# Loading q of the attention in one array over all partitions, q and k by token halves, and sharing the k split between engines

## The chip, the core and the metric

The kernel runs on one core of one Trainium2 chip. The metric is the device time of one execution in microseconds (us), lower is better; runs of a changed kernel are taken beside runs of the kernel before on the same chip, and a ratio below 1 means faster. The engines are TensorE (PE in the profile, PEld for its weight loads), VectorE (DVE), ScalarE (ACT), GpSimd (POOL) and SyncE (SP), which here only issues DMAs.

## The reference

One decoder block over 2048 tokens and 1024 channels, in float32. What matters here:

```python
proj = x @ w_in + b_in          # q, k, v for 3 head groups of 8 heads of 64; gates; LRU input; merge gates
q, k = rope(q), rope(k)
for g, (window, dilation) in enumerate(((128, 1), (512, 4), (2048, 16))):
    o_g, lse_g = dilated_band_attention(q[:, :, g], k[:, :, g], v[:, :, g], window, dilation)
attn = sum over g of softmax(lse)_g * o_g;   y_a = (attn * silu(g_attn)) @ w_attn_proj
y_b  = (rg_lru(causal_conv(u)) * silu(g_lru)) @ w_lru_proj
out  = (sigmoid(gA) * y_a + sigmoid(gB) * y_b) @ w_out + b_out
x    = layer_norm(alpha * x + out)
```

In `dilated_band_attention` the tokens are regrouped by their residue modulo the dilation, and each block of 128 queries meets the keys of its own block and of the block before it, under a band mask.

## The kernel before, in words

There are three stages, and all of them share the DMA queue that SP feeds.

**Stage A, the projection** (to 1473 us in the profile). The plan has 72 entries, two token halves times 36 pairs of 128 output features. All but the first entry of each half are computed by seven block products (`product`, line 595), one for each tick; a tick is 12 matmuls of 512 columns and 2.7 us of PE. Every fp32 operand is split in a rounded part (ACT) and a remainder (DVE or POOL), so a product needs three matmuls for each block. Raw weights are loaded by SP (lines 218 and 298 and others), the remainders of the weights are stored in the first half (`wl_scr`) and loaded again in the second (line 278). Finished tiles go through generators, "chains", which are resumed tick by tick while a budget for each engine lasts. `qk_chain` applies the rotary embedding and writes k to `k_scr` (line 315) and q, scaled and split, to `qh_scr` and `ql_scr` (line 326 for group 2, whose tokens are regrouped by 16, line 329 for the others). `v_chain` transposes v and writes it to `v_scr` (line 358 and those around it). For each of 12 units (a group `g` and a head pair `hp`) the arrays `qh`, `ql` and `k` are [128, 2048], the first head in rows 0 to 63, the second in rows 64 to 127.

**Stage B, the attention** (1473 to about 1804 us). `unit(u)` takes the groups in the order 0, 2, 1 for each head pair. Each of 12 units has 16 steps, 192 in all. In loop step `m` the kernel issues `step_s(m)` (scores `s`, line 966, then the masked row minimum on DVE, line 970, and exp on ACT, line 972), `step_t(m-3)` (transposes, line 981, copied out by ACT or DVE, lines 986 and 988) and `step_v(m-4)` (times V, line 1005). The result goes to `o_scr` from ACT's DMA queue every four steps. Scores have three PSUM buffers, so `step_s(3)` waits for the exp input of step 0 to have been read.

The operands of a unit are prepared by `unit_parts(u)`:

- `A` is q: for head `h` one half of the partitions holds the rounded part and the other the remainder. It takes four loads (`q_part`, line 798) of 64 partitions with 8 KB each.
- `C` (named `b2` in the code) receives k, one load of 64 partitions for each head (`k_part`, line 777); its other partitions stay zero (memsets on POOL, lines 773 and 774, in units 0 and 1).
- `B` (`B1`) gets the rounded k in both halves of the partitions, two copies, and `C` keeps the remainder, one subtraction. This "split" is done for each head and each half of the tokens, [64, 1024] each. Only for head 0 of unit 0 do ACT (lines 781 and 782) and DVE (line 788) do it; everything else is done by POOL (lines 785, 786, 788).

A function `later(n, fn)` puts work off by n ticks or steps; the splits come 3 and 4 after the load. `first` is `unit_parts(0)`, `second` is `unit_parts(1)`, `firstv` is `v_parts(0, 0)`, the V of group 0 for the first two head pairs. In the last entry of stage A, whose seven ticks are j = 0 to 6, these loads are issued as the buffers of stage A come free: k of unit 0 at j = 2, q at j = 3, V at j = 4, k of unit 1 at j = 5 and 6. After stage A come the rest of `second` and the V of group 2; from then on one load is issued for each step, those of unit u+1 from the first step of unit u on (`loads`).

The order on each engine is the order in which the program issues. The layer below gives the DMAs of SP and ACT in turn one of eight counters, and a DMA waits until the one before it on its counter has landed. So SP, which works in order, can be held by a DMA that was issued eight places earlier, and that may be one of ACT's.

**Stage C, the combination and the output projections**, follows and is not touched.

Of the kernel before, what the change touches and what calls it, by code (L numbers as in the profile page):

```python
# [8 lines left out]
F32 = mybir.dt.float32  # L9
# [6 lines left out]
P = 128  # L16
S = 2048
# [3 lines left out]
CH = 512  # L21
# [10 lines left out]
def hybrid_block_kernel(ctx: ExitStack, tc: tile.TileContext, a: dict, out: bass.AP):  # L32
    nc = tc.nc
    sp, act, dve, pool, pe = nc.sync, nc.scalar, nc.vector, nc.gpsimd, nc.tensor

    def flat(t):
        return t.bitcast(F32)


    dram = ctx.enter_context(tc.tile_pool(name="dram", bufs=1, space=DRAM))  # L40
# [5 lines left out]
    mg_scr = dram.tile([2 * D, S], F32, name="mg_scr")  # L46
    yb_scr = dram.tile([D, S], F32, name="yb_scr")

    v_scr = [[dram.tile([S, 260], F32, name=f"v_scr{g}{j}") for j in range(2)] for g in range(3)]

    qk_scr = {(n, u): dram.tile([P, S], F32, name=f"{n}_scr{u}") for u in range(12) for n in ("qh", "ql", "k")}


    wl_scr = [dram.tile([P, 7, CH], F32, name=f"wl_scr{p}") for p in range(36)]
# [32 lines left out]
    def later(lag, fn):  # L87
        late.append((now["n"] + lag, fn))
# [201 lines left out]
    def qk_chain(rw, f, c):  # L290
        isq = f < FT_K
        u = f % 12
        g = u // 4
        nm = f"{f}_{c}"
        yield Ask(need=1)
        sw = take("sw" + nm)
        for b in range(4):
            sp.dma_start(flat(sw)[32 * b:32 * b + 32], flat(rw)[32 * (b ^ 1):32 * (b ^ 1) + 32])
        yield Ask(lag=2, DVE=1.2 if c < 2 else 1.0, POOL=1.7)
        cos, sin = CS[c % 2]  # L300
        tt(dve, flat(rw), flat(rw), cos, ALU.mult)
        tt(pool, flat(sw), flat(sw), sin, ALU.mult)
        yield Ask(lag=1, need=1 if g else 0, DVE=1.2 if g else 1.0)
        if g == 0:
            rp = rw
            tt(dve, flat(rp), flat(rw), flat(sw), ALU.add)
            give(sw)
        else:
            rp = take("rp" + nm)
            v, r = "p (j r) -> p j r", 4 if g == 1 else 16  # L310
            tt(dve, blocks(flat(rp), g), flat(rw).rearrange(v, r=r), flat(sw).rearrange(v, r=r), ALU.add)
            give(rw, sw)
        if not isq:
            yield Ask()
            sp.dma_start(qk_scr["k", u][:, c * CH:(c + 1) * CH], flat(rp))
            give_sent(rp)
            return
        yield Ask(need=1, ACT=.66, DVE=.9)
        hi = take("hi" + nm)
        act.activation(hi, flat(rp), AF.Copy, scale=0.125)  # L320
        dve.scalar_tensor_tensor(out=rp, in0=flat(rp), scalar=0.125, in1=flat(hi), op0=ALU.mult, op1=ALU.subtract)
        yield Ask()
        for t, part in ((hi, "qh"), (rp, "ql")):
            dst = qk_scr[part, u]
            if g == 2:
                sp.dma_start(dst.rearrange("p (r i) -> p r i", r=16)[:, :, 32 * c:32 * c + 32],
                             flat(t).rearrange("p (r i) -> p r i", r=16))
            else:
                sp.dma_start(dst[:, c * CH:(c + 1) * CH], flat(t))
        give_sent(hi, rp)  # L330


# [6 lines left out]
    def v_chain(vt, sgn, f, c):  # L339
        g, hp = divmod(f - FT_V, 4)  # L340
        st = {}

        def turn():
            tp = st["tp"] = ps.tile([P, 4, P], F32, tag="t", name=f"vtp{f}_{c}", bufs=2)
            for b in range(4):
                pe.transpose(tp[:, b, :], flat(vt)[:, b * P:(b + 1) * P], ident)  # L346
            give(vt)

        yield Ask(cond=lambda: tog["n"] < 2)
        tog["n"] += 1  # L350
        pe_later(2, turn)
        yield Ask(lag=3, cond=lambda: len(vs_free) > 0, ACT=.66)
        vs = vs_free.pop(0)
        act.activation(vs[:, :, 1:129], st["tp"], AF.Copy, scale=sgn)
        tog["n"] -= 1
        yield Ask()
        dst = v_scr[g][hp // 2][c * CH:(c + 1) * CH, (hp % 2) * 130:(hp % 2) * 130 + 130]
        sp.dma_start(dst.rearrange("(b p) f -> p b f", p=P), vs)
        vs_free.append(vs)


# [315 lines left out]
    for s, pl in enumerate(plan):  # L677
        if pl[0] and pl[4] == "ug":
            i = pl[1][1][0] - FT_U
# [69 lines left out]
    lo_, up_ = slice(0, 64), slice(64, P)  # L749
# [5 lines left out]
    units = {}  # L755
# [5 lines left out]
    def unit_parts(u):  # L761

        sl = USLOT[u % 2]
        g, hp = unit(u)
        q = {n: qk_scr[n, 4 * g + hp] for n in ("qh", "ql", "k")}

        def k_part(h, hs, os):
            def fn():
                if h == 0:
                    units[u] = [None, big(sl[1], [P, 2, S], F32R, f"B{u}")]  # L770
                    if u < 2:
                        B2[u] = big(sl[2], [P, 2, S], F32R, f"C{u}")
                        pool.memset(flat(B2[u][up_, 0]), 0.0)
                        pool.memset(flat(B2[u][lo_, 1]), 0.0)
                    units[u].append(B2[u % 2])
                _, B1, b2 = units[u]
                sp.dma_start(flat(b2[hs, h]), q["k"][hs])

                def split(t):
                    if (u, h) == (0, 0):  # L780
                        act.activation(B1[hs, h, t], flat(b2[hs, h, t]), AF.Copy)
                        act.activation(B1[os, h, t], flat(B1[hs, h, t]), AF.Copy)
                        eng = dve
                    else:
                        pool.tensor_copy(B1[hs, h, t], flat(b2[hs, h, t]))
                        pool.tensor_copy(B1[os, h, t], flat(B1[hs, h, t]))
                        eng = pool
                    eng.tensor_tensor(out=b2[hs, h, t], in0=flat(b2[hs, h, t]), in1=flat(B1[hs, h, t]), op=ALU.subtract)

                later(3, lambda: split(slice(0, S // 2)))  # L790
                later(4, lambda: split(slice(S // 2, S)))
            return fn

        def q_part(hs, h, n, qs):
            def fn():
                if (hs, h) == (lo_, 0):
                    units[u][0] = big(sl[0], [P, 2, S], F32R, f"A{u}")
                sp.dma_start(flat(units[u][0][hs, h]), q[n][qs])
            return fn

        return [k_part(0, lo_, up_), k_part(1, up_, lo_), q_part(lo_, 0, "qh", lo_), q_part(up_, 0, "ql", lo_),
                q_part(lo_, 1, "ql", up_), q_part(up_, 1, "qh", up_)]

    VT = {}

    def v_parts(g, j):
        src = v_scr[g][j]

        def part(i):
            def fn():  # L810
                if i == 0:
                    VT[g, j] = big(VSLOT[g, j], [P, 16, 260], F32, f"V{g}{j}")
                V = VT[g, j]
                if g == 0:
                    sp.dma_start(V[:, 4 * i:4 * i + 4], src[i * CH:(i + 1) * CH].rearrange("(n p) f -> p n f", p=P))
                elif g == 1:
                    sp.dma_start(V[:, 4 * i:4 * i + 4], src[i * CH:(i + 1) * CH].rearrange("(j r) f -> j r f", r=4))
                else:
                    sp.dma_start(V[:, 4 * i:4 * i + 4], src.rearrange("(i r) f -> i r f", r=16)[:, 4 * i:4 * i + 4])
            return fn  # L820

        return [part(i) for i in range(4)]
# [72 lines left out]
    first, second, firstv = unit_parts(0), unit_parts(1), v_parts(0, 0)  # L895
    low = NS
    where = [(s, j) for s in range(NQ) for j in range(ticks[s])]
    for T, (s, j) in enumerate(where):
        now["n"] = T
        for k in ("PE", "ACT", "DVE", "POOL"):  # L900
            left[k] = min(left[k], 0.0) + LEN
        if plan[s][2]:
            spend(**COST[plan[s][2][j]])
        product(s, j)
        for fn in events.pop(T, []):
            fn()
        run(late)
        run_chains()
        if s == NQ - 1:
            for fn in ((), (), first[:2], first[2:], firstv, second[:1], second[1:2])[j]:  # L910
                fn()
        evacuate(s, j)
        low = min(low, len(vacant))
        if TRACE:
            print(T, s, j, plan[s][4], len(vacant), len(lo_vacant), len(chains), {k: round(v, 1) for k, v in left.items()})
    n = len(where)
# [111 lines left out]
    def split(h, l, r, scale=None, eng=dve):  # L1028
        if scale is None:
            act.activation(h, r, AF.Copy)  # L1030
            eng.tensor_tensor(out=l, in0=r, in1=flat(h), op=ALU.subtract)
        else:
            act.activation(h, r, AF.Copy, scale=scale)
            dve.scalar_tensor_tensor(out=l, in0=r, scalar=scale, in1=flat(h), op0=ALU.mult, op1=ALU.subtract)
# [18 lines left out]
        later(1 if c else 2, lambda: split(t[:, 0], t[:, 1], r, eng=eng))  # L1053

    NB = 12 * 16
    for fn in second[2:] + v_parts(2, 0):
        fn()
    VORD = {0: (1, 0), 4: (0, 1), 5: (2, 1), 6: (1, 1)}
    loads = []
    for m in range(NB + 4):  # L1060
        u, n = divmod(m, 16)
# [142 lines left out]
    for n in range(32):  # L1204
        c, f = divmod(n, 8)
# [201 lines left out]
```

## Time and profile before

| | |
|---|---|
| runs | 2287.06 us median of 3 (2281.97 to 2290.84) |
| profiled execution | 2284.91 us |
| its span, first to last instruction | 2282.8 us |
| mean granted TensorE clock | 0.988 |
| PE, PEld busy | 2219.8 us (97%), 1870.6 us (82%) |
| DVE, ACT, POOL busy | 1743.3 us (76%), 1094.8 us (48%), 872.3 us (38%) |
| moved by DMA | 515.53 MB, mean 226 GB/s |

The busy share is an average over three stages. PE is the engine with the least idle time in stages A and B, so what matters is where PE is idle or slowed there, and what ended each of those waits. "Granted clock" is the share of full speed at which PE was allowed to run in a stretch.

### The profile page before, as it was taken

To read this page: it belongs to the slowest core of one execution; us is meant where nothing else is said; L and a number is where in the kernel's file an instruction comes from. 1 tells how busy PE (TensorE), PEld (TensorE's weight loads), DVE (VectorE), ACT (ScalarE), POOL (GpSimd) and SP (SyncE) were. 2 spreads that over 40 slices of the span, in tenths; PEclk is the share of its full clock that TensorE was granted. 3 is DMA by queue.
4 is the path that set the end of the run, shared out by engine and by line. 5 is a ranking of instruction groups with operands and counts; after the bars stand their busy time and mean duration, and the time that the engine had idled before them with its cause. 6 is when DMAs were issued, how large, how long until landed. Compare 5 with 4: busy or idle time off the path is not lost.

```text
span 2282.8 us, 34216 instructions
## 1 busy us (share of the span) xinstructions
PE 2219.8 (97%) x11008; PEld 1870.6 (82%) x11008; DVE 1743.3 (76%) x3228; ACT 1094.8 (48%) x1979; POOL 872.3 (38%) x640
## 2 busy tenths in 40 slices
PE   7999999999999999999999999989999999989998
PEld 6888878888888788888888888889999877768886
DVE  8787988999898777777878878656666578747677
ACT  5344545555455555565576565556666511121100
POOL 1544554556553012212312312465766256512220
PEclk9999999999999999999999999999999999999999
DMA  7998988988988777777777876995976589864431
GB/s 229 264 265 249 246 258 243 284 256 265 276 253 287 240 209 223 208 221 228 223 212 225 246 218 221 259 242 140 259 206 159 167 267 297 272 213 162 157 120 65
DMA packets 327443, 515.53 MB, mean 226 GB/s; under 512 B 96864, under 2 KB 137824, under 8 KB 322656
## 3 DMA queue, kind: packets, MB, share of 16 engines
q1 hardware_dynamic: 296352, 468.30, 66.5%
q0 software_dynamic: 10080, 18.35, 5.0%
q10 hardware_dynamic: 20832, 26.68, 3.6%
q8 instruction: 88, 1.44, 0.3%
q14 instruction: 91, 0.75, 0.1%
HBM read 307.89 MB, written 180.16 MB: 214 GB/s over the span
## 4 chain that ended last, share of the span: by engine, by line
PE 75%; DMA 7%; DVE 7%; issue 6%; ACT 2%; POOL 2%; SPq 1%; ACTq 0%; DVEq 0%; POOLq 0%
PE q L595 55%; PE o L1005 4%; PE s L966 3%; PE pt L981 2%; DMA A<-qh_scr 2%; PE z L1287 1%; PE z L1286 1%; PE z L1285 1%; PE yb L1194 1%; PE yb L1195 1%; PE yb L1193 1%; POOL me L1259 1%; PE vtp L346 1%; ACT p L972 1%; PE g L467 1%
## 5 line engine op out<-in xcount | busy, mean ns | idle before, releaser
L595 PE MATMUL q<-xT,hS 128*128 128x512 f32 x1680 | 521.1, 392 | 6.0 <-ACT e L618 6.0
L595 PE MATMUL q<-xT,l 128*128 128x512 f32 x1120 | 437.2, 390 | 0.0
L595 PE MATMUL q<-xB,hA 128*128 128x512 f32 x1248 | 389.5, 394 | 9.9 <-ACT xB L199 5.8
L595 PEld LDWEIGHTS q<-xT,hS 128*128 128x128 f32 x1680 | 315.1, 188 | 71.5 <-ACT e L618 6.4
L595 PE MATMUL q<-xB,l 128*128 128x512 f32 x904 | 354.0, 392 | 0.0
L595 PEld LDWEIGHTS q<-xB,hA 128*128 128x128 f32 x1248 | 235.2, 189 | 60.3 <-ACT xB L199 5.8
L595 PEld LDWEIGHTS q<-xT,l 128*128 128x128 f32 x1120 | 210.8, 188 | 44.4
L972 ACT ACTIVATE p<-p,osb 128x256 f32<-128x256 f32 (+1 forms) x384 | 156.6, 455 | 117.5 <-DVE osb L970 116.6
L211 POOL TENSOR_TENSOR S<-S,wA 128x512 f32<-128x512 f32 x35 | 45.7, 1305 | 424.4 <-DVE S L211 300.9
L970 DVE CUSTOM_DVE_ANT_0 p<-s,mask 128x256 f32<-128x256 f32 (+1 forms) x384 | 125.5, 364 | 101.8 <-PE s L966 65.5
L595 PEld LDWEIGHTS q<-xB,l 128*128 128x128 f32 x904 | 170.7, 189 | 36.2 <-DVE l L211 0.3
L211 POOL TENSOR_TENSOR sw<-sw,sin 128x512 f32<-128x512 f32 x96 | 160.2, 1675 | 65.4 <-DMA sw<-y 64.6
L595 PE MATMUL q<-xB,hS 128*128 128x512 f32 x560 | 173.9, 392 | 3.0 <-DVE v L211 3.0
L595 PE MATMUL q<-xT,hA 128*128 128x512 f32 x560 | 173.0, 390 | 1.5 <-ACT hi L320 1.3
L1005 PE MATMUL o<-V,ptb 128*128 128x65 f32 x1200 | 166.8, 278 | 7.4 <-ACT ptb L986 4.1
L1005 PEld LDWEIGHTS o<-V,ptb 128*128 128x128 f32 x1200 | 154.0, 197 | 18.5 <-ACT ptb L986 14.9
L256 ACT ACTIVATE hA<-wA 128x512 fp32r<-128x512 f32 x218 | 135.6, 624 | 68.1 <-DMA wA<-in_w_in_dram 21.3
L256 ACT ACTIVATE hS<-S 128x512 fp32r<-128x512 f32 x175 | 109.2, 624 | 102.3 <-DVE S L211 56.6
L211 POOL TENSOR_TENSOR l<-wA,hA 128x512 fp32r<-128x512 f32 x68 | 106.3, 1563 | 81.6 <-ACT hA L256 64.9
L966 PE MATMUL s<-B,A 128*128 128x256 f32 (+1 forms) x384 | 118.6, 330 | 8.3 <-DMA A<-qh_scr 5.7
L595 PEld LDWEIGHTS q<-xT,hA 128*128 128x128 f32 x560 | 104.8, 188 | 24.4 <-ACT hi L320 1.7
L595 PEld LDWEIGHTS q<-xB,hS 128*128 128x128 f32 x560 | 104.1, 188 | 24.7 <-issue 3.8
(196 smaller groups left out, 4843.7 us busy)
## 6 DMA issues: line engine op xcount, KB each, us to landing
wA<-in_w_in_dram SPq DMA_DIRECT2D x253, 256.0 KB, 4.9
wl_scr<-l SPq DMA_DIRECT2D x105, 512.0 KB, 5.2
l<-wl_scr SPq DMA_DIRECT2D x105, 512.0 KB, 4.5
sw<-y SPq DMA_DIRECT2D x384, 64.0 KB, 3.1
wS<-in_w_in_dram SPq DMA_DIRECT2D x70, 256.0 KB, 4.6
wS<-in_w_in_dram POOLq DMA_DIRECT2D x70, 256.0 KB, 6.6
o_scr<-osb ACTq DMA_DIRECT2D x48, 264.0 KB, 5.5
oc<-o_scr SPq DMA_DIRECT2D x48, 264.0 KB, 5.3
```

Source lines behind the costliest of these rows:

```text
L211: eng.tensor_tensor(out=out, in0=in0, in1=in1, op=op)
L256: act.activation(h, r, AF.Copy)
L346: pe.transpose(tp[:, b, :], flat(vt)[:, b * P:(b + 1) * P], ident)
L467: pe.matmul(g, gw[:, 1, j], vh, start=False, stop=True)
L595: pe.matmul(bank, w[:, ks], x[:, kk, xx], start=(first and i == 0), stop=(last and i == 11))
L966: pe.matmul(s[:, h, (0 if g == 2 and n else lo):256], q, k, start=(i == 0), stop=(i == 1))
L970: dve.tensor_tensor_reduce(out=p[:, h, lo:256], in0=s[:, h, lo:256], in1=mask[:, lo:256], scale=1.0, scalar=3e38, op0=ALU.add, op1=ALU.min ...
L972: act.activation(p[:, h, lo:256], p[:, h, lo:256], AF.Exp, scale=-1.0, bias=mm)
L981: pe.transpose(pt[:, 2 * h + x, :], p[:, h, x * P:(x + 1) * P], ident)
L1005: pe.matmul(o[:, n % 2, h * 65:h * 65 + 65], ptb[:, 2 * h + x, :], V[:, kb, vo + h * 65:vo + h * 65 + 65], start=(x == lo // P), stop=(x = ...
L1193: pe.matmul(yb, WL[f][:, 0, k], xx[:, 0], start=(k == 0), stop=False)
L1194: pe.matmul(yb, WL[f][:, 0, k], xx[:, 1], start=False, stop=False)
```

## The change

Three arrays and their loads are laid out anew, and the loads before stage B are issued in another order.

- q of a unit is one array `q_scr[u]` of [2, 128, 2048]: for each head the 128 rows as `A` wants them. `qk_chain` writes each tile into two row groups of 64. The rounded part goes to groups 0 and 3, the remainder to groups 1 and 2. For group 2 that takes two DMAs for each tile, one for each head, where it was one.
- `q_part(h, t)` loads all 128 partitions of one head and one half of the tokens (4 KB in each partition), four loads for each unit as before. `k_part(h, t)` loads one head and one half of the tokens, so k takes four loads where it took two. All of the first half of the tokens of k come first, then the second half, then q in the same order.
- The split of a half follows its own load by 3, and for both of the first two units ACT and DVE do head 0, both halves.
- V of group 0 is kept as [128, 16, 260], by key within the block and block, so that a load of four blocks is 4160 contiguous bytes in each partition, where it was four pieces of 1040.
- In the last entry of stage A the first loads start at j = 1, and k of unit 1 is issued between the V loads of unit 0.

```diff
-    v_scr = [[dram.tile([S, 260], F32, name=f"v_scr{g}{j}") for j in range(2)] for g in range(3)]
+    v_scr = [[dram.tile([S, 260] if g else [P, 16, 260], F32, name=f"v_scr{g}{j}") for j in range(2)] for g in range(3)]
-    qk_scr = {(n, u): dram.tile([P, S], F32, name=f"{n}_scr{u}") for u in range(12) for n in ("qh", "ql", "k")}
+    k_scr = [dram.tile([P, S], F32, name=f"k_scr{u}") for u in range(12)]
+    q_scr = [dram.tile([2, P, S], F32, name=f"q_scr{u}") for u in range(12)]
...
         for t, part in ((hi, "qh"), (rp, "ql")):
-            dst = qk_scr[part, u]
+            dst = q_scr[u].rearrange("h (x d) s -> (h x) d s", x=2)
+            dst = dst[0:4:3] if part == "qh" else dst[1:3]
             if g == 2:
-                sp.dma_start(dst.rearrange("p (r i) -> p r i", r=16)[:, :, 32 * c:32 * c + 32],
-                             flat(t).rearrange("p (r i) -> p r i", r=16))
+                src = flat(t).rearrange("p (r i) -> p r i", r=16)
+                for h in range(2):
+                    sp.dma_start(dst[h].rearrange("d (r i) -> d r i", r=16)[:, :, 32 * c:32 * c + 32],
+                                 src[64 * h:64 * h + 64])
             else:
-                sp.dma_start(dst[:, c * CH:(c + 1) * CH], flat(t))
+                sp.dma_start(dst[:, :, c * CH:(c + 1) * CH], flat(t))
...
-        def k_part(h, hs, os):
+        def k_part(h, t):
+            hs, os = ((lo_, up_), (up_, lo_))[h]
...
-                sp.dma_start(flat(b2[hs, h]), q["k"][hs])
-
-                def split(t):
-                    if (u, h) == (0, 0):
+                sp.dma_start(flat(b2[hs, h, t]), k[hs, t])
+
+                def split():
+                    if u < 2 and h == 0:
                         act.activation(B1[hs, h, t], flat(b2[hs, h, t]), AF.Copy)
                         act.activation(B1[os, h, t], flat(B1[hs, h, t]), AF.Copy)
                         eng = dve
...
-                later(3, lambda: split(slice(0, S // 2)))
-                later(4, lambda: split(slice(S // 2, S)))
+                later(3, split)
...
-        def q_part(hs, h, n, qs):
+        def q_part(h, t):
...
-                sp.dma_start(flat(units[u][0][hs, h]), q[n][qs])
+                sp.dma_start(flat(units[u][0][:, h, t]), q[h][:, t])
...
-        return [k_part(0, lo_, up_), k_part(1, up_, lo_), q_part(lo_, 0, "qh", lo_), q_part(up_, 0, "ql", lo_),
-                q_part(lo_, 1, "ql", up_), q_part(up_, 1, "qh", up_)]
+        T2 = (slice(0, S // 2), slice(S // 2, S))
+        return [k_part(h, t) for t in T2 for h in range(2)] + [q_part(h, t) for t in T2 for h in range(2)]
...
-                    sp.dma_start(V[:, 4 * i:4 * i + 4], src[i * CH:(i + 1) * CH].rearrange("(n p) f -> p n f", p=P))
+                    sp.dma_start(V[:, 4 * i:4 * i + 4], src[:, 4 * i:4 * i + 4])
...
-            for fn in ((), (), first[:2], first[2:], firstv, second[:1], second[1:2])[j]:
+            for fn in ((), first[:2], first[2:6], first[6:] + firstv[:1], firstv[1:2] + second[:2], firstv[2:3] + second[2:4], firstv[3:])[j]:
...
-    for fn in second[2:] + v_parts(2, 0):
+    for fn in second[4:] + v_parts(2, 0):
```

More of the change, by code (lines that the diff above doesn't have):

```diff
@@ L314, in qk_chain @@
             yield Ask()
-            sp.dma_start(qk_scr["k", u][:, c * CH:(c + 1) * CH], flat(rp))
+            sp.dma_start(k_scr[u][:, c * CH:(c + 1) * CH], flat(rp))
             give_sent(rp)
@@ L356, in v_chain @@
         yield Ask()
-        dst = v_scr[g][hp // 2][c * CH:(c + 1) * CH, (hp % 2) * 130:(hp % 2) * 130 + 130]
-        sp.dma_start(dst.rearrange("(b p) f -> p b f", p=P), vs)
+        fs = slice((hp % 2) * 130, (hp % 2) * 130 + 130)
+        if g == 0:
+            dst = v_scr[g][hp // 2][:, 4 * c:4 * c + 4, fs]
+        else:
+            dst = v_scr[g][hp // 2][c * CH:(c + 1) * CH, fs].rearrange("(b p) f -> p b f", p=P)
+        sp.dma_start(dst, vs)
         vs_free.append(vs)
@@ L764, in unit_parts @@
         g, hp = unit(u)
-        q = {n: qk_scr[n, 4 * g + hp] for n in ("qh", "ql", "k")}
-        def k_part(h, hs, os):
+        k, q = k_scr[4 * g + hp], q_scr[4 * g + hp]
+        def k_part(h, t):
+            hs, os = ((lo_, up_), (up_, lo_))[h]
             def fn():
-                if h == 0:
+                if (h, t) == (0, T2[0]):
                     units[u] = [None, big(sl[1], [P, 2, S], F32R, f"B{u}")]
@@ L788, in split @@
                     eng.tensor_tensor(out=b2[hs, h, t], in0=flat(b2[hs, h, t]), in1=flat(B1[hs, h, t]), op=ALU.subtract)
-                later(3, lambda: split(slice(0, S // 2)))
-                later(4, lambda: split(slice(S // 2, S)))
+                later(3, split)
             return fn
-        def q_part(hs, h, n, qs):
+        def q_part(h, t):
             def fn():
-                if (hs, h) == (lo_, 0):
+                if (h, t) == (0, T2[0]):
                     units[u][0] = big(sl[0], [P, 2, S], F32R, f"A{u}")
-                sp.dma_start(flat(units[u][0][hs, h]), q[n][qs])
+                sp.dma_start(flat(units[u][0][:, h, t]), q[h][:, t])
             return fn
-        return [k_part(0, lo_, up_), k_part(1, up_, lo_), q_part(lo_, 0, "qh", lo_), q_part(up_, 0, "ql", lo_),
-                q_part(lo_, 1, "ql", up_), q_part(up_, 1, "qh", up_)]
+        T2 = (slice(0, S // 2), slice(S // 2, S))
+        return [k_part(h, t) for t in T2 for h in range(2)] + [q_part(h, t) for t in T2 for h in range(2)]
     VT = {}
```

## The prediction

> **What bounds the kernel now.** I read the chain of waits first. It says that PE carries 75% of the span and that 2% of it, some 45 us, is q being loaded for the attention.
>
> ```profile
> PE 75%; DMA 7%; DVE 7%; issue 6%; ACT 2%; POOL 2%; SPq 1%; ACTq 0%; DVEq 0%; POOLq 0%
> ```
>
> Then the stretches of stages A and B, from the third row on one for each unit of the attention, cut at about its first score (stretch, busy time of PE, PEld, DVE, ACT, POOL with instruction counts, granted clock, DMA share, GB/s).
>
> ```profile
> core 0: us, PE busy (x) PEld busy (x) DVE busy (x) ACT busy (x) POOL busy (x), PEclk, DMA share, GB/s
> 50.00:770.00 720.00, 711.34 (x3166) 585.86 (x3165) 625.37 (x780) 357.73 (x595) 354.26 (x263) 1.00 0.88 261
> 770.00:1464.00 694.00, 694.00 (x3102) 574.50 (x3102) 540.96 (x746) 418.80 (x681) 150.93 (x104) 1.00 0.74 224
> 1473.00:1503.00 30.00, 27.33 (x211) 26.82 (x209) 18.64 (x77) 18.89 (x42) 18.57 (x13) 0.89 1.05 254
> 1503.00:1533.00 30.00, 24.68 (x183) 23.43 (x182) 13.69 (x79) 14.08 (x43) 17.07 (x13) 0.89 0.86 248
> 1533.00:1565.00 32.00, 29.05 (x208) 28.16 (x209) 16.81 (x77) 17.63 (x44) 23.01 (x16) 0.84 0.58 144
> 1565.00:1594.00 29.00, 28.75 (x249) 28.07 (x249) 18.24 (x76) 19.27 (x43) 17.67 (x12) 1.00 0.58 145
> 1594.00:1617.00 23.00, 22.50 (x191) 21.54 (x190) 14.24 (x81) 14.63 (x44) 17.62 (x12) 1.00 0.97 237
> 1617.00:1642.00 25.00, 24.34 (x206) 23.06 (x205) 16.50 (x77) 17.38 (x44) 16.29 (x12) 1.00 0.93 294
> ```
>
> In stage A PE is full in the second half and idle for 8.7 us in the first, where DVE is at 87%. In stage B units 3, 4 and 5 show what groups 0, 2 and 1 cost undisturbed: 249 matmuls in 29 us, 191 in 23 us, 206 in 25 us. Units 0, 1 and 2 do the same kinds of work at a worse rate. By those rates their 211, 183 and 208 matmuls would take 24.6, 22.0 and 25.2 us; they took 30, 30 and 32. So the first three units lose 5.4, 8.0 and 6.8 us, 20.2 us together, partly as idle PE and partly as a clock of 0.84 to 0.89. Four waits of PE lie in them:
>
> ```profile
> 1476.33 0.45 PE L966 MATMUL s<-B,A 128*128 128x128 f32 x1 [2.67 <-DMA A<-qh_scr]
> 1505.58 0.33 PE L966 MATMUL s<-B,A 128*128 128x128 f32 x1 [2.56 <-POOL B L786]
> 1508.00 0.48 PE L966 MATMUL s<-C,A 128*128 128x128 f32 x1 [2.09 <-POOL C L788]
> 1535.88 0.30 PE L966 MATMUL s<-B,A 128*128 128x128 f32 x1 [3.04 <-DMA A<-qh_scr]
> ```
>
> The idle sums to 10.4 us; the rest of the 20.2 is PE at half clock after each wait. The chain of waits, in order of time, says what made the operands late:
>
> ```profile
> 1464.40 11.83 DMA A<-qh_scr
> 1478.70 10.92 DMA C<-k_scr
> 1518.59 9.46 DMA o_scr<-osb
> 1528.56 7.24 DMA A<-qh_scr
> ```
>
> Unit 0 waits for q, whose last load is issued at 1464.40 and lands at 1476.23. Unit 1 waits for POOL, which begins with its k at 1489.74 and ends the fourth split at 1507.95:
>
> ```profile
> 1489.74 1.03 POOL L785 CAST B<-C 64x1024 fp32r<-64x1024 f32 x1 [10.80 <-DMA C<-k_scr]
> 1505.61 2.34 POOL L788 TENSOR_TENSOR C<-C,B 64x1024 fp32r<-64x1024 f32 x1
> ```
>
> Unit 2's q is held back because SP's next load waits for a store of unit 0's result by ACT (the 9.46 us) on the same counter. Under all three lies the rate of the loads:
>
> ```profile
> 1470.00:1472.00 2.00, 2.00 (x11) 1.65 (x10) 2.00 (x2) 1.97 (x2) 2.00 (x2) 1.00 1.02 221
> 1502.00:1504.00 2.00, 1.02 (x10) 0.88 (x8) 1.38 (x6) 0.91 (x2) 2.00 (x2) 1.00 1.04 407
> ```
>
> Both stretches have the DMA engines full. At 1470 q is arriving in 64 partitions, at 221 GB/s; at 1502 V of group 2, in 128 partitions, at 407 GB/s.
>
> **The change, part by part.**
>
> *q over 128 partitions.* The 2 MB of a unit cost 9.5 us at 221 GB/s and 5.2 us at 407. I take 407: that transfer has 4160 bytes in each of 128 partitions, the new one 4096. If it stays at 221, q gains nothing.
>
> *Unit 0's start.* When the transfers may begin is set by stage A's buffers:
>
> ```profile
> 1457.20 1.13 SPq L777 DMA_DIRECT2D C<-k_scr  x2
> 1462.64 0.45 SPq L798 DMA_DIRECT2D A<-qh_scr  x1
> 1467.21 11.39 SPq L815 DMA_DIRECT2D V<-v_scr  x4
> ```
>
> k is issued at 1457.20, on the end of the first product of the last entry, and q at 1462.64, on the end of the third. Issuing earlier in the program changes neither. k (1 MB, 64 partitions, 4.7 us) is through by about 1465, as now, with the last weight remainder, now behind two k loads, still 5 us ahead of its product. From 1465 on the 2 MB of q and a store take 5.8 us: the first halves land by about 1468.5, all of q by 1471.7 with a us from the last byte to the signal, instead of 1476.23. PE can go on at 1473.1 with the scores of steps 0 to 2, and the 2.67 us go.
>
> *The new wait.* Head 0 of unit 1 goes to ACT and DVE, and its two splits stand in both queues before the first row minimum and the first exp of unit 0. Both engines work in order, so the attention can't begin before k of unit 1 (head 0, second half) has landed. That load waits on its counter for the last part of q (1471.7), and three parts of V and two of k are ahead of it in the queue: with the part itself that is 1.6 MB at 407 and 0.79 MB at 221, 3.9 and 3.6 us, and a 0.25 MB store of ACT, 0.6 us. From 1471.7 that gives a landing at 1480; I allow 1477 (the queue runs ahead of my counting) to 1484. Then come these durations:
>
> ```profile
> 1463.49 1.06 ACT L781 ACTIVATE B<-C 64x1024 fp32r<-64x1024 f32 x1 [0.96 <-DMA C<-k_scr]
> 1468.69 3.09 DVE L788 TENSOR_TENSOR C<-C,B 64x1024 fp32r<-64x1024 f32 x1
> 1472.90 1.21 DVE L788 TENSOR_TENSOR C<-C,B 64x1024 fp32r<-64x1024 f32 x1
> 1477.03 0.29 DVE L970 CUSTOM_DVE_ANT_0 p<-s,mask 128x128 f32<-128x128 f32 x1 [2.31 <-PE s L966]
> ```
>
> One copy of 1.06 us and one subtraction, 1.21 us (3.09 where it met POOL's own at 1468), bring the first row minimum to 1482.5 to 1484.5, against 1477.03 now. PE has done steps 0 to 2 by then and lacks only step 3, which saves about 1 us. So unit 0 goes 5 us later than now (2 to 9), with PE idle for some 8 us from 1474.6 and at half clock after it, as it is now. Two stretches show how long that lasts:
>
> ```profile
> 1480.00:1484.00 4.00, 4.00 (x28) 4.00 (x26) 2.33 (x13) 2.74 (x7) 0.00 (x0) 0.69 1.10 237
> 1536.00:1546.00 10.00, 10.00 (x52) 9.61 (x53) 4.44 (x24) 4.60 (x13) 9.60 (x8) 0.55 1.00 233
> ```
>
> After 1476.33 the clock was back during the stretch from 1480 to 1484 (0.69), some 6 us on. After 1535.88 it was 0.55 for 10 us. I take the first for the new wait, which is within unit 0's present loss, and the second as a bound, 2 us worse. The Trainium skill (TensorE: Matmul & The Clock Gate, "What's actually happening") has the clock halved after an idle window of about 3.4 us and restored after a busy one of the same length. The trace agrees on the half clock and shows longer returns; by the page an estimate of the loss would be 1.7 us a time. I use the rows.
>
> *Unit 1's stall.* Its four splits were POOL's, 18.2 us from 1489.74. Now POOL has two, after 1477, and is done by about 1487, while unit 1 begins at about 1508. The 8.0 us go; cover 20 us.
>
> *Unit 2's stall.* The counters now pair unit 2's q with loads and with the store after step 7, not the one after step 15, and its first k halves need only unit 0's ninth step. q can land by about 1520; unit 2 begins near 1531. The 6.8 us go; cover about 10 us.
>
> *V of group 0.* Pieces of 4160 for 1040 bytes save perhaps 1 us of a queue that no longer decides: nothing on the path. The other units have no wait for operands: nothing.
>
> *Stage A.* SP issues 32 more DMAs, half as large, for group 2's q. A row of SP gives them 0.55 us each, 18 us over 1400, and each takes a counter.
>
> ```profile
> L326 SPq DMA_DIRECT2D qh_scr<-hi x16: 524/551/619, 97.5 to 1321.2; - x16
> ```
>
> PE's waits in stage A are few and all behind ACT and DVE:
>
> ```profile
> PE q L595 <- ACT e L618: 6.0, 1, 6.0
> ACT vs L354 <- DMA v_scr<-vs: 28.0, 7, 9.4
> ```
>
> The first of these two rows is one wait of 6 us, the second says that ACT is at times held by a late store. I put the stores at +1 us, between -1 (other counters fall better) and +6 (one more such wait).
>
> *Sum.* 2284.91 (profiled execution; span 2282.8) - 8.0 - 6.8 + 5 + 1 = 2276.1 us. The median of the runs, 2287.06, is 2.15 above the profiled one, so on that scale **2278 us**, 0.4% less. About 0.5%, 11.4 us, is what a measurement of this kernel can tell from no change.
>
> **Rivals.**
>
> *Slower: the rounded q's store is carried by few DMA engines and stage A waits.* The store of `hi` for groups 0 and 1 now writes an array whose outermost dimension is 2. If a transfer is shared out by that dimension, two of the 16 engines carry 128 KB each: at 407/16 = 25.4 GB/s that is 5.2 us where 16 engines take 0.65, and whatever is queued behind lands up to 4.5 us later. There are 32 such stores, 16 in the first half, where DVE is at 87%. For it: the ACT row above, stores already hold ACT. Against it: PE has four PSUM buffers of 2.7 us each ahead of DVE, and in the second half nothing is short. If each of the 16 costs PE 0.6 us, the gain of 9 us is gone; at 1.4 us (22 us in all) the change is slower by over 0.5%; I price this end at 2300. With a loss of 3 to 20 us it ends between 2281 and 2298. No transfer of before has so small an outer dimension, so the trace can't decide. The Trainium skill states such a rule (DMA: Bandwidth & Descriptors, "Why a DMA increments its semaphore by 16 and not by 1"): the number of engines is the largest, up to 16, that divides the slowest dimension on both sides; that would be 2 here. No run here shows it yet.
>
> *ACT and DVE are held longer.* If q stays at 221 GB/s, or stores get between, k of unit 1 lands 4 us or more later and the attention with it; unit 1's and 2's gains stay: 2282 to 2287. For it: the loads on 64 partitions of a full queue landed 11 us after issue. Against it: the 407 GB/s.
>
> *The stalls move less than I say.* If unit 2's q is held by a counter after all, 6.8 us stay: 2285, with the previous rival's price.
>
> **How the numbers follow.** Forecast (gain 5 to 17): 0.52, with 0.25 of it above 11.4 us, when k of unit 1 lands by 1477 or the half clock is short. Later k or a stall that stays (gain 0 to 5): 0.13. Few engines, with a loss of 3 to 20 us: 0.18; with more: 0.17. So faster by over 0.5% is 0.25, within it 0.58, slower 0.17. The range of 8 in 10 runs from 2269 (a gain of 18, over which I put 0.05) to 2296, which leaves out about 0.13 of the slow end.
>
> **What would show it.** In the profile after: loads of A near 400 GB/s; the first score of unit 0 without a wait for A; PE idle from about 1475 to 1483, ended by DVE, and ACT and DVE waiting for k just before; no wait of PE at units 1 and 2, which take 22 to 23 and 25 to 26 us. Wrong it would be if stage A ends later than 1473 by several us, with waits behind `q_scr` or with the stores of `hi` landing in about 10 us instead of 5.3; or if PE still waits for B, C or A after unit 0.
>
> ```profile
> qh_scr<-hi SPq DMA_DIRECT2D x48, 256.0 KB, 5.3
> ```

## The result, and the profile after

| | before | after |
|---|---|---|
| median of 4 runs | 2286.13 us (2281.97 to 2290.84) | 2318.48 us (2316.84 to 2323.63) |
| profiled execution, its span | 2284.91, 2282.8 us | 2317.63, 2315.9 us |
| mean granted clock | 0.988 | 0.986 |

The ratio is 1.0138 (1.0117 to 1.0158): 1.4% slower, where 0.4% faster was forecast. The time lies outside the range.

The first view to read is where stage B begins and ends. This is the group of all score matmuls, whose two last times are its first and last start, before and then after:

```profile
L966 PE MATMUL s<-B,A x384: 220/308/562, 1473.3 to 1800.5; 128*128 128x256 f32 x168, 128*128 128x128 f32 x24
```

```profile
L976 PE MATMUL s<-B,A x384: 272/305/583, 1510.8 to 1830.9; 128*128 128x256 f32 x168, 128*128 128x128 f32 x24
```

Stage A ends 37.5 us later. From the first to the last score it is 327.2 us before and 320.1 after, 7.1 less; from there to the end of the span 482.3 and 485.0, 2.7 more. 37.5 - 7.1 + 2.7 is the 33.1 us by which the spans differ. The part that only stores what the attention reads lost five times what the attention gained, and even that gain is not all the change's: in four profiles of kernels further down whose attention reads its operands in the same number of loads as before, in the same order, it takes 321.2 to 326.3.

The chain of waits of after has PE at 53% where it was 75%, with DMA at 9%. The share of PE in this chain says little by itself (the kernel with 64 more stores, further down, is 0.14% slower than before and has 47%), so what follows rests on the stretches and on single waits:

```profile
PE 53%; DMA 9%; issue 6%; DVE 6%; ACT 2%; SPq 1%; POOL 1%; ACTq 0%; DVEq 0%; POOLq 0%
```

The stretches of after (columns as in the prediction): the two halves of stage A, a store of the rounded q, and units 0 to 2.

```profile
48.00:770.00 722.00, 697.48 (x3072) 572.18 (x3071) 606.53 (x746) 345.37 (x575) 347.91 (x262) 0.99 0.86 251
770.00:1500.00 730.00, 720.43 (x3199) 594.34 (x3198) 569.33 (x782) 431.95 (x703) 153.77 (x107) 0.99 0.73 223
...
1403.66:1405.66 2.00, 2.00 (x11) 1.65 (x10) 1.97 (x4) 1.16 (x2) 1.15 (x1) 1.00 1.07 350
1407.66:1411.16 3.50, 3.50 (x17) 2.92 (x16) 3.47 (x5) 3.40 (x5) 2.50 (x2) 1.00 0.13 37
...
1510.85:1548.20 37.35, 26.27 (x206) 25.91 (x206) 20.13 (x76) 22.32 (x45) 13.79 (x8) 0.82 0.83 273
1548.20:1570.70 22.50, 21.99 (x185) 20.93 (x184) 13.77 (x77) 14.08 (x43) 16.70 (x11) 1.00 0.52 166
1570.70:1596.40 25.70, 25.16 (x212) 23.82 (x212) 16.95 (x79) 17.95 (x45) 18.91 (x14) 1.00 0.57 187
```

PE is idle for 24.5 us in the first half, where it was 8.7, and for 9.6 in the second, where it was full: 25.4 us more. The clock is 0.99 in both, where it was 1.00, and that is the other 12 us of the 37.5: by the record of the granted clock, PE ran at half speed in six stretches of stage A, 27.3 us in all, each just behind a wait of PE of 2.7 to 6.1 us or begun within it. Half of that time is lost, 13.7 us; before there was one such stretch, 3.4 us, for 1.7. Unit 0 takes 37.4 us, and units 1 and 2 take 22.5 and 25.7, their undisturbed time.

The fourth row is the cause, seen directly. A store of `hi` was issued just before it:

```profile
1405.66 0.57 SPq L334 DMA_DIRECT2D q_scr<-hi  x1
```

From 1407.66 on, for 3.5 us, the DMA engines are busy to 0.13 and move 37 GB/s. Two of 16 engines are 0.125. The queue had been full until then (1.07); now two engines work and 14 are idle. By the packets of the trace, 12 or 13 of the 32 stores of `hi` for groups 0 and 1 (by how closely the share is bounded) are followed, within 14 us, by 1.5 us or more at such a share; behind the others other transfers keep it higher. In the profile of before that happens behind none of the 48 stores of `hi`.

The trace also counts the engines. Every DMA of the kernel before steps its counter 16 times when it lands, 31072 steps for 1942 DMAs. In the changed kernel 416 steps are missing, and all steps fall in place, none ahead of its DMA's issue, if each of these 32 stores has 3 steps: one for each of two engines, and one for the other 14 together. No other store lacks any, not the remainder's either, whose two row groups lie side by side. Counted so, these stores land 9.5 us after their issue (median), where it was 5.3; "about 10" was the prediction's sign for this rival.

Who pays, in the waits of stage A of after, from 48 to 1470 us (in total, times, longest):

```profile
ACT hA L258 <- DMA wA<-in_w_in_dram: 41.9, 18, 9.4
...
DVE y L213 <- DMA sw<-y: 29.4, 11, 6.6
...
PE q L604 <- DVE v L213: 7.6, 4, 6.1
PE q L604 <- DVE u L213: 6.9, 3, 5.0
...
PE q L604 <- ACT si L398: 4.4, 1, 4.4
PE q L604 <- DMA l<-wl_scr: 3.8, 2, 3.1
```

Those who wait are not the ones that store. Weights, their remainders and `sw` are issued behind the store and land late: those that SP issued within 8 us behind one of the 32 stores landed 7.6 us after issue on average, where it was 4.7 before; all others landed after 4.1 us in both kernels. DVE and ACT wait for them, and PE for DVE and ACT. The same two waits for a DMA were shorter before:

```profile
ACT hA L256 <- DMA wA<-in_w_in_dram: 19.8, 12, 5.9
...
DVE y L211 <- DMA sw<-y: 8.9, 8, 2.5
```

At unit 0 the new wait is there (after, in order of time):

```profile
1515.65 1.06 ACT L792 ACTIVATE B<-C 64x1024 fp32r<-64x1024 f32 x1 [6.79 <-DMA C<-k_scr]
...
1520.00 1.06 ACT L792 ACTIVATE B<-C 64x1024 fp32r<-64x1024 f32 x1 [1.46 <-DMA C<-k_scr]
1521.08 2.00 DVE L799 TENSOR_TENSOR C<-C,B 64x1024 fp32r<-64x1024 f32 x1 [2.38 <-ACT B L792]
1523.01 0.27 DVE L980 CUSTOM_DVE_ANT_0 p<-s,mask 128x128 f32<-128x128 f32 x1
1523.56 0.58 PE L976 MATMUL s<-B,A 128*128 128x256 f32 x1 [11.08 <-DVE osb L980]
```

ACT waits for k of unit 1, DVE for ACT, the first row minimum for DVE, and PE is idle for 11.08 us. No wait of PE for `A`, `B` or `C` is left in the attention.

### The profile page after: what moved, and what is told of

Same layout as the page of the kernel before. It is cut to its first block, busy times and chain, and to the rows that moved or that the text cites. A ratio compares the mean times of both kernels' runs of the same rounds, so it can differ in the third digit from the quotient of the medians.

```text
span 2315.9 us, 34291 instructions
## 1 busy us (share of the span) xinstructions
PE 2225.1 (96%) x11008; PEld 1867.9 (81%) x11008; DVE 1752.1 (76%) x3230; ACT 1097.2 (47%) x1983; POOL 861.2 (37%) x634
## 4 chain that ended last, share of the span: by engine, by line
PE 53%; DMA 9%; issue 6%; DVE 6%; ACT 2%; SPq 1%; POOL 1%; ACTq 0%; DVEq 0%; POOLq 0%
PE q L604 30%; PE o L1015 5%; PE s L976 3%; PE pt L991 2%; PE yb L1204 2%; PE yb L1205 2%; PE yb L1203 2%; PE z L1297 1%; PE z L1295 1%; PE z L1296 1%; DMA v_scr<-vs 1%; POOL me L1269 1%; DMA l<-wl_scr 1%; DMA A<-q_scr 1%; DMA C<-k_scr 1%
## 5 line engine op out<-in xcount | busy, mean ns | idle before, releaser
L604 PEld LDWEIGHTS q<-xT,hA 128*128 128x128 f32 x560 | 105.5, 189 | 32.4 <-issue 8.2
L213 DVE TENSOR_TENSOR y<-y,cos 128x512 f32<-128x512 f32 x96 | 105.8, 1108 | 29.5 <-DMA sw<-y 29.4
```

The costliest lines, as they stand in the source:

```text
L213: eng.tensor_tensor(out=out, in0=in0, in1=in1, op=op)
L604: pe.matmul(bank, w[:, ks], x[:, kk, xx], start=(first and i == 0), stop=(last and i == 11))
```

## Experiments: is it the two engines?

Four kernels, one batch. The first two ask whether the outermost dimension of 2 is enough to explain the loss, from both sides: taken out of the changed kernel, and put into the kernel before.

**Rounded q in two stores.** The changed kernel, with

```diff
+            elif part == "qh":
+                for h in range(2):
+                    sp.dma_start(dst[h][:, c * CH:(c + 1) * CH], flat(t)[64 * h:64 * h + 64])
             else:
                 sp.dma_start(dst[:, :, c * CH:(c + 1) * CH], flat(t))
```

> The changed kernel, but the rounded q of groups 0 and 1 goes out in two stores of 64 rows instead of one with an outermost dimension of 2. If few DMA engines carry that one store, stage A comes back: the first score at 1470 to 1480 us (1510.9 in the changed kernel), time 2278 to 2286. If the loss of stage A comes from group 2's stores in halves or from the new pairing of the counters, it stays at 2310 or more (32 further DMAs would make that worse).

Measured: 2284.41 us (2283.65 to 2288.26), ratio to before 0.9997 (0.9984 to 1.001). The 34 us are gone with one more DMA for each store, the same bytes and the same destination rows.

**The store alone, in the kernel before.** The rounded q of groups 0 and 1 goes to an array of N row groups, one row longer than they need to be, so that the rows can't be merged into one dimension. Here N is 2:

```diff
+    qhp = [dram.tile([2, 65, S], F32, name=f"qhp{u}") for u in range(8)]
...
+            elif part == "qh":
+                sp.dma_start(qhp[u][:, 0:64, c * CH:(c + 1) * CH], flat(t))
```

> The kernel before, with the suspected cost alone: the rounded q of groups 0 and 1 is stored in an array of [2, 65, 2048], so that the store has an outermost dimension of 2; number and sizes of the DMAs are as before. If few engines carry it: first score at 1500 to 1515 us, time 2315 to 2330. If not: 2287 give or take 5, first score at 1473.

Measured: 2319.02 us (2316.54 to 2323.89), ratio 1.0141 (1.0118 to 1.0163). Nothing else of the change is in this kernel, and its time is that of the changed kernel. That the two agree so closely is partly chance: stage A loses 31.5 us here and 37.5 there, and there the attention gives some of it back. Its scores:

```profile
L973 PE MATMUL s<-B,A x384: 219/306/562, 1504.8 to 1831.1; 128*128 128x256 f32 x168, 128*128 128x128 f32 x24
```

They begin 31.5 us later than before. Of that 19.6 us are idle PE and 11.8 half clock. And the same two waits of stage A, as long as in the changed kernel:

```profile
ACT hA L258 <- DMA wA<-in_w_in_dram: 40.6, 16, 8.1
...
DVE y L213 <- DMA sw<-y: 28.9, 12, 8.2
```

**The same with 32 row groups of 4.** `[32, 5, S]`, `qhp[u][:, 0:4, ...]`: the rows are cut up more, but the outermost dimension divides by 16.

> As pad2, but [32, 5, 2048], an outermost dimension of 32. If it is the number of engines that counts, this is the kernel before: 2287 give or take 5. If it is a store in row groups as such, or where its rows lie in memory, it is slow like pad2.

Measured: 2288.44 us (2283.36 to 2296.39), ratio 1.0014 (0.9997 to 1.003), first score at 1475.0. Row groups as such cost nothing that can be seen.

**Group 2's halves.** The kernel before, with the two stores for each tile of group 2 that the change has:

```diff
             if g == 2:
-                sp.dma_start(dst.rearrange("p (r i) -> p r i", r=16)[:, :, 32 * c:32 * c + 32],
-                             flat(t).rearrange("p (r i) -> p r i", r=16))
+                for hs in (slice(0, 64), slice(64, P)):
+                    sp.dma_start(dst[hs].rearrange("p (r i) -> p r i", r=16)[:, :, 32 * c:32 * c + 32],
+                                 flat(t)[hs].rearrange("p (r i) -> p r i", r=16))
```

> The kernel before, with group 2's q stored in halves of 64 partitions, 32 more DMAs, and nothing else. If few engines are the cause of stage A's loss: 2287 give or take 6. If group 2's halves or the counters are: 2300 or more.

Measured: 2287.35 us (2281.14 to 2295.33), ratio 1.0002 (0.9986 to 1.0019). The 32 further DMAs are not the loss.

**Four and eight groups.** If the outermost dimension sets the number of engines, the loss must fall with it. `[4, 33, S]` and `[8, 17, S]`:

> As the run with the outermost dimension of 2, but the rounded q of groups 0 and 1 goes to an array whose outermost dimension is 4 (4 row groups of 32). If the outermost dimension sets how many of the 16 DMA engines carry a store, each store takes twice as many engines and half as long (some 2.6 us instead of 5.2): a loss of 4 to 16 us against before, 2290 to 2303, and stretches with the engines' share at 0.25 instead of 0.13. If only 2 is special, or the row groups as such cost, it is 2286 or 2318.

> The same with an outermost dimension of 8 (8 row groups of 16). Engines by the outermost dimension: some 1.3 us a store where 16 engines take 0.65, a loss of 0 to 5 us, 2286 to 2292. If the loss does not go with the number of engines, 2318.

Measured: 2301.49 us (2299.29 to 2303.77), ratio 1.0062 (1.0044 to 1.008), for 4, and 2309.6 (2308.14 to 2317.74), 1.0105 (1.0084 to 1.0126), for 8. By the whole time the second expectation is missed: 8 groups are worse than 4. The profile says why this is no verdict on the store. The scores of 4 groups, and a stretch behind its store issued at 1382.31:

```profile
L975 PE MATMUL s<-B,A x384: 220/306/561, 1486.5 to 1812.4; 128*128 128x256 f32 x168, 128*128 128x128 f32 x24
```

```profile
1383.80:1386.30 2.50, 2.50 (x12) 2.07 (x11) 2.47 (x4) 2.07 (x3) 0.98 (x1) 1.00 0.27 61
```

The scores of 8 groups, a stretch behind its store issued at 1376.40, and the longest wait of PE in its attention:

```profile
L975 PE MATMUL s<-B,A x384: 220/308/562, 1480.6 to 1821.7; 128*128 128x256 f32 x168, 128*128 128x128 f32 x24
```

```profile
1378.40:1379.40 1.00, 1.00 (x6) 0.84 (x5) 0.96 (x2) 1.00 (x1) 0.00 (x0) 1.00 0.43 129
```

```profile
PE s L975 <- DMA A<-qhp: 17.5, 5, 6.4
```

Stage A, where the stores are, ends 31.5, 13.2, 7.3 and 1.7 us later than before for 2, 4, 8 and 32 groups (one execution each; the kernel with group 2's halves, of the same time as before, has 4.7, so the last two are near the spread), and the plateau is at 0.13, 0.27 and, for a us, 0.43: the order that the number of engines asks for. The count of steps is sharper than the plateau: of each store it has 3, 5, 9 and 16 for 2, 4, 8 and 32 groups, that is 2, 4 and 8 engines with one step for the rest, and then all 16. The stores land 9.5, 7.3, 5.9 and 4.6 us after issue (medians). What 8 groups lose besides is in the attention, because this kernel reads q back in 4 loads of 16 partitions for each one of before, and PE waits 17.5 us for them. The read side was mine to add, and should have been left at one load; the whole time of that run doesn't measure the store.

## Experiments: what the rest of the change is worth

**Unit 1's head 0 back on POOL.** With two stores the time came out at that of before, not 8 us below it, and its profile had the wait of PE at unit 0 (9.8 us). So, on top of the two stores:

```diff
-                    if u < 2 and h == 0:
+                    if u < 1 and h == 0:
```

> The changed kernel with the rounded q of groups 0 and 1 stored in two DMAs of 64 rows, and head 0 of unit 1 split by POOL again, as before; unit 0 keeps ACT and DVE. If the wait of PE at unit 0 (9.8 us in the run with two stores) comes from those splits standing ahead of the first row minimum, it goes: unit 0 takes 25 to 30 us instead of 36.0, unit 1 stays at 22 to 23 because POOL, beginning near 1482 with 18.2 us of work, is done before unit 1 begins, and the kernel ends 6 to 10 us earlier than the run with two stores (2284.4): 2274 to 2279, 0.3 to 0.5% faster than before. If the wait is the arrival of q, not the splits, or if unit 1 then waits for POOL, the sum stays at 2282 to 2287.

Measured: 2274.24 us (2272.48 to 2279.21), ratio 0.9947 (0.993 to 0.9963): faster than both kernels, by 0.5% and 1.9%. Units 0 to 2 of this run:

```profile
1480.50:1505.20 24.70, 24.02 (x206) 23.43 (x206) 16.24 (x74) 18.02 (x40) 19.92 (x13) 1.00 1.02 348
1505.20:1527.80 22.60, 22.06 (x184) 20.87 (x184) 13.74 (x78) 14.16 (x43) 16.00 (x12) 1.00 0.72 231
1527.80:1553.50 25.70, 25.23 (x212) 23.85 (x212) 16.91 (x79) 17.80 (x45) 20.55 (x15) 1.00 0.57 186
```

24.7, 22.6 and 25.7 us at full clock: the undisturbed 24.6, 22.0 and 25.2 that the prediction worked out. Of the 20.2 us that were to be had, 18.7 are there (91.7 before by the starts of the units, 73.0 now). The profile of before is at the long end, though: in the four others with its loads (outermost dimensions 2 and 32, group 2's halves, and 64 more stores below) units 0 to 2 take 86.5 to 90.9 us, so the gain by units is 13.5 to 18.7. Giving ACT and DVE unit 1's splits bought nothing and cost unit 0 its start.

**The price of more stores.** In the run with two stores the first score came at 1481.9 and in the one just shown at 1480.5, not at 1473.3. The kernel before, with 64 more stores of half the size (group 2's as above, and the rounded q of groups 0 and 1 in halves of 64 rows):

> The kernel before, with the three kinds of store that the run with two stores has in halves (group 2's rounded q and remainder, and the rounded q of groups 0 and 1): 64 more DMAs of SP in stage A, stage B as before. In the run with two stores the first score began 8.6 us later than before (1481.9 against 1473.3). If that is the price of the 64 DMAs and their counters, this kernel takes 2290 to 2297, 0.3 to 0.5% slower than before, with the first score at 1478 to 1484. If the 8.6 us are the spread of single executions, 2285 to 2289 and a ratio within 0.1% of 1.

Measured: 2290.8 us (2287.78 to 2296.14), ratio 1.0014 (1.0002 to 1.0026): 0.5 to 6 us by the interval. The time is at the low edge of the first expectation, and the ratio, 0.14%, lies between the two. Its profiled execution had the first score at 1484.1, 10.8 us later than before. So the halves of the stores have a small price, and the start of the attention in one execution shows more of it than the median does (its attention then took 5.7 us less, though nothing was changed there). How large it is stays open within that interval.

**The old stores, with half-width loads.** Would the order and the halves of the tokens have done without the new layout of q? On top of unit 1 on POOL, `qh` and `ql` are stored as before, and each load of q becomes two of 64 partitions:

```diff
-                sp.dma_start(flat(units[u][0][:, h, t]), q[h][:, t])
+                hs = (lo_, up_)[h]
+                sp.dma_start(flat(units[u][0][lo_, h, t]), q[h][hs, t])
+                sp.dma_start(flat(units[u][0][up_, h, t]), q[1 - h][hs, t])
```

> The rounded q and its remainder in two arrays of 128 rows, stored as in the kernel before (one DMA each, all groups), and each half of q read in two loads of 64 partitions, some 9.5 us for the 2 MB of a unit; all else as in the run with unit 1 on POOL (halves of the tokens, order, V of group 0). Stage A then has the DMAs of before: its first score comes at 1473 to 1477. If the gain of the attention comes from the halves of the tokens, their order and the counters, units 0 to 2 stay near 24.7, 22.6 and 25.7 us and it ends at 2266 to 2272, earlier than the run with unit 1 on POOL (2274.2). If it comes from q over 128 partitions, the stalls at units 0 to 2 come back, 10 to 18 us: 2278 to 2288.

Measured: 2281.57 us (2277.08 to 2283.92), ratio 0.9979 (0.9964 to 0.9993). It is 7.3 us behind the run with unit 1 on POOL, although its stage A ends 3.8 us earlier. Its scores, and the waits of PE from 1470 to 1560:

```profile
L974 PE MATMUL s<-B,A x384: 220/306/561, 1476.7 to 1797.7; 128*128 128x256 f32 x168, 128*128 128x128 f32 x24
```

```profile
PE s L974 <- DMA A<-ql_scr: 4.8, 1, 4.8
PE s L974 <- DMA A<-qh_scr: 1.3, 1, 1.3
```

Its units 0 to 2 take 25.8, 27.3 and 32.4 us, 11.4 us more at units 1 and 2. Both waits are for unit 2's q, on the two sides of its start (1529.75 and 1531.76). SP issued that q only at 1524.67, after standing 6.5 us behind a store of `o_scr` on the same counter; it then came in at 250 GB/s (1528 to 1532). So the new layout of q pays, and more than its extra stores cost. But this kernel has twice as many loads of q, which fall on other counters, and the run does not part the width of a load from the number of loads. The Trainium skill (DMA: Bandwidth & Descriptors, "Rules for kernel authors") says that two transfers to the two halves of the partitions serialize, and that one over 128 should be used. The runs agree with the advice, by 7.3 us for this kernel; that the two serialize no run here shows.

**V of group 0 as before.** On top of unit 1 on POOL, `v_scr` of group 0 is `[S, 260]` again, stored and loaded by rows.

> The run with unit 1 on POOL, with V of group 0 in the rows and pieces of the kernel before (1040 bytes). If this part of the change is worth nothing on the path, 2272 to 2277, as that run (2274.2) within 0.15%. If the pieces of 4160 bytes are what brings V early enough at unit 0, its first products with V wait, 3 to 8 us: 2277 to 2282.

Measured: 2273.59 us (2271.42 to 2274.71), ratio 0.9948 (0.9933 to 0.9963), and units 0 to 2 again take 24.7, 22.6 and 25.7 us. V by key and block is worth nothing here, as predicted.

## Why the prediction was wrong

**The step that failed** is the term for stage A: +1 us, between -1 and +6. It measured +37.5. That term priced SP's further DMAs; those of group 2 cost nothing that can be seen (ratio 1.0002), all 64 of the run with two stores some 0.5 to 6 us. What it left to a rival was the shape of the store, and that was nearly the whole effect: 31.5 of the 37.5 us with nothing else changed. The rival named the mechanism as it is: outermost dimension 2, two of 16 engines, transfers behind it late, stage A waiting. I gave it 0.35 and priced its end at 2300, and it came out at 2318. Three of its steps were too small:

- It counted 16 stores in the first half, at up to 1.4 us, and held that in the second half nothing is short. PE lost 15.8 us of idle in the first half and 9.6 in the second. Over all 32 stores the kernel with only this cost loses 31.5 us in stage A, 1.0 us a store.
- It held PE's four PSUM buffers for cover. But several inputs of DVE and ACT are late here (the two rows of waits for `wA` and `sw`), and PE waited up to 6.1 us at a time in spite of the buffers.
- It priced idle PE alone. A third of the loss, 12 us, is PE at half clock behind those waits.

The Trainium skill's rule (DMA: Bandwidth & Descriptors, "Why a DMA increments its semaphore by 16 and not by 1") has the number of engines as the largest up to 16 that divides the slowest dimension on both sides. The runs agree: 0.13 of the engines at 2, 0.27 at 4, 0.43 of a short stretch at 8, no loss at 32, and steps of the counters for 2, 4, 8 and 16 engines. I had the rule, and a store whose rows could be read off the diff; the right weight for a stated rule that a shape in the diff meets exactly was more than 0.35.

**The rest held, with sizes off.**

- q at 407 GB/s and unit 0 without its wait for `A`: near enough. While unit 0's q was arriving the queue moved 360 to 411 GB/s, and PE has no wait for `A`:

```profile
1506.00:1508.00 2.00, 2.00 (x10) 1.68 (x9) 1.02 (x2) 0.07 (x1) 1.96 (x2) 1.00 0.95 386
```

- The new wait of unit 0: its place and its chain are as written, ACT and DVE behind k of unit 1. I had k landing 6.9 us after PE could begin with the scores (1480 against 1473.1), and it was 9.2 (1520.0 against 1510.8). PE was idle for 11.08 us, not 8, and unit 0 lost 8.1 us, not 5, against its 29.3 in the profile of before; the stated bounds were 2 to 9. (The four other profiles with the loads of before have 26.6 to 29.3.)
- The half clock behind it: I took 6 us for its return. After 1523.56 the clock was back during the stretch from 1527 to 1531, by the record of the clock at 1528.9, 5.3 us on:

```profile
1523.00:1527.00 4.00, 3.44 (x16) 3.44 (x17) 3.71 (x22) 3.53 (x10) 3.86 (x3) 0.50 1.02 395
1527.00:1531.00 4.00, 4.00 (x30) 4.00 (x29) 1.42 (x6) 2.35 (x6) 0.53 (x1) 0.76 1.00 382
```

- Unit 1's and unit 2's stalls: -7.3 and -6.9 us, for -8.0 and -6.8 in the sum. That each size comes out so well is partly luck. The two units take 62.4 us together in the profile of before and 59.2 to 63.3 in the four others with its loads, and unit 2 takes 25.7 to 25.9 in three of those: where the stall for its q falls differs from one to the other. With the change they take 48.1 to 48.3 in three profiles, so together 11 to 15 us are gone.
- V of group 0: nothing, as said.

Without the failed step the forecast would have stood within 7 us: with two stores the kernel takes 2284, for 2278 forecast. But the gain of 9 us that was forecast is not there either (ratio 0.9997, 0.9984 to 1.001). In the profile of that run units 1 and 2 gain 14.3 us, for 14.8 in the sum; unit 0 loses 6.7, for 5; and the first score comes 8.6 us later, for 1. So what is missing lies mostly in stage A again, where the price of the stores' halves, 0.5 to 6 us, is known only within those bounds.

## What to carry to other kernels

Read the outermost dimension of each DMA on both sides, after adjacent rows are merged, before anything else in a change of layout: where it is 2, two engines carry the transfer, and everything queued behind it is late, also for engines that have nothing to do with it. Splitting such a store into one DMA for each group costs little; here it gave back 34 us. And before work is moved to a faster engine, see what stands behind it in that engine's order: a split that POOL had time for held the first row minimum of another unit for 11 us.

## What was not expected of the hardware

A store of 256 KB confined to two engines costs stage A about 1.0 us on average, although in the second half of stage A the queues were busy to only 0.74 on average before and PE was full. The mean share of the queues is therefore no measure of slack. It fell from 0.88 to 0.86 and from 0.74 to 0.73 while the loss grew to 37 us, so neither half's average would have raised suspicion; only stretches of a few us at 0.13 show it.
